# Row-wise infinity norm of an 8192 x 8192 matrix: another cut of the rows into transfers, and another way out for the results

## The chip, the cores and the metric

The kernel runs on one core of a Trainium2 chip; the other cores are idle. The metric is the device time of one execution in microseconds, and the number compared is the median of several executions. A separate execution is recorded by the hardware profiler; all durations below are from that one.

## The reference

```python
def setup_inputs():
    return {
        "x": np.random.randn(8192, 8192).astype(np.float32),
    }

def reference(x: np.ndarray) -> np.ndarray:
    return np.linalg.norm(x, ord=np.inf, axis=1)
```

With `axis=1` the infinity norm of a row is the largest absolute value in it. So 268.4 MB are read, one maximum is taken over each row of 8192 numbers, and 8192 numbers (32 KB) are written.

## The kernel before

The 8192 rows are laid over the 128 partitions of SBUF, so that each partition holds 64 rows ("row slots" below). They come in groups `g` of 256 rows, and partition `p` of a group holds rows `2p` and `2p+1` of it: the view `x_g` (line 53) makes these two rows one run of 16384 numbers (64 KB, contiguous in DRAM). In this text a column is one float32 in each of the 128 partitions, 512 bytes in all; the input has 524288 columns.

`_pieces` cuts these columns into 47 transfers: 25 whole pairs of rows (16384 columns), then, from the list `TAIL`, eight single rows (8192), and fourteen pieces that shrink from 6400 to 1408 columns. A piece never crosses a pair, but it may cross the border between the two rows of one.

Every piece is one DMA, issued by SyncE (line 81), into a ring of three pairs (`RING`, 49152 columns). A piece that doesn't fit before the ring's end starts at 0 again. The framework makes the DMA wait until the reduces that read the old contents of its place are done. In the program as built, the DMAs take eight completion semaphores in turn, so a DMA also waits for the landing of the one that last used its semaphore.

VectorE takes the pieces in the same order. `absmax` (line 66) is one `tensor_reduce` with maximum of absolute values. Whole rows in a piece give their result straight to `res`; a part of a row gives a partial maximum to `part`, and when the row's last part is in, a second small `tensor_reduce` (line 98) joins the partial results into `res`.

When the last pair but one is done (line 103), the 62 results of each partition are brought into DRAM order: for each of the two rows of a pair, TensorE transposes 31 columns of `res` into PSUM with the identity (line 108), ScalarE copies them to `o_sb` (line 109), and ScalarE issues two stores (lines 111 and 112). The results of the last pair go straight from `res` to DRAM at the very end, by a store on SyncE's queue (line 113): 128 partitions with 8 bytes each.

No order is written out by hand other than that of the program text; each engine runs its own list, and semaphores join the lists.

Of the kernel before, what the change touches and what calls it, by code (L numbers as in the profile page):

```python
# [1 line left out]

# [5 lines left out]

P = 128
FP32 = mybir.dt.float32  # L10

TAIL = (
    [8192] * 8
    + [6400, 5888, 4096]
    + [4992, 4544, 3776, 3072]
    + [3264, 2944, 2624, 2304, 2112, 1728, 1408]
)
RING = 3 * 16384  # L20


def _pieces(total, n_cols, pair):

    tail = sum(TAIL)
    assert (total - tail) % pair == 0
    cuts = [(a, a + pair) for a in range(0, total - tail, pair)]
    at = total - tail
    for w in TAIL:
        end = at + w  # L30
        while at < end:
            e = min(end, (at // pair + 1) * pair)
            cuts.append((at, e))
            at = e
    return cuts


@with_exitstack
def kernel(
    ctx: ExitStack,  # L40
    tc: tile.TileContext,
    x: bass.AP,
    out: bass.AP,
):
    nc = tc.nc
    n_rows, n_cols = x.shape
    R = 2
    pair = R * n_cols
    G = n_rows // (P * R)
    total = n_rows // P * n_cols  # L50


    x_g = x.rearrange("(g p r) m -> g p (r m)", p=P, r=R)
    out_g = out.rearrange("(g p r) -> g p r", p=P, r=R)

    single = ctx.enter_context(tc.tile_pool(name="single", bufs=1))
    psum_pool = ctx.enter_context(tc.tile_pool(name="psum", bufs=1, space=bass.MemoryType.PSUM))

    ring = single.tile([P, RING], FP32)
    res = single.tile([P, G, R], FP32)  # L60
    part = single.tile([P, G * R, 8], FP32)
    ident = single.tile([P, P], FP32)
    make_identity(nc, ident)

    def absmax(dst, src):
        nc.vector.tensor_reduce(  # L66
            out=dst, in_=src, axis=mybir.AxisListType.X,
            op=mybir.AluOpType.max, apply_absolute_value=True,
        )

    n_part = {}
    flushed = False
    at = 0
    for a, b in _pieces(total, n_cols, pair):
        w = b - a
        if at + w > RING:
            at = 0
        g = a // pair
        buf = ring[:, at : at + w]
        at += w  # L80
        nc.sync.dma_start(out=buf, in_=x_g[g, :, a - g * pair : b - g * pair])
        s = a
        while s < b:
            row = s // n_cols
            if s % n_cols == 0 and b - s >= n_cols:
                k = (b - s) // n_cols
                absmax(
                    res[:, g, row % R : row % R + k],
                    buf[:, s - a : s - a + k * n_cols].rearrange("p (k m) -> p k m", m=n_cols),
                )  # L90
                s += k * n_cols
                continue
            e = min(b, (row + 1) * n_cols)
            i = n_part.get(row, 0)
            n_part[row] = i + 1
            absmax(part[:, row, i : i + 1], buf[:, s - a : e - a])
            if e == (row + 1) * n_cols:
                nc.vector.tensor_reduce(  # L98
                    out=res[:, g, row % R : row % R + 1], in_=part[:, row, : i + 1],
                    axis=mybir.AxisListType.X, op=mybir.AluOpType.max,  # L100
                )
            s = e
        if b == (G - 1) * pair and not flushed:
            flushed = True
            o_sb = single.tile([G - 1, P, R], FP32)
            for r in range(R):
                o_ps = psum_pool.tile([G - 1, P], FP32, name=f"o_ps{r}")
                nc.tensor.transpose(o_ps, res[:, : G - 1, r], ident)  # L108
                nc.scalar.copy(o_sb[:, :, r], o_ps)  # L109
            h = (G - 1) // 2 + 1  # L110
            nc.scalar.dma_start(out=out_g[:h], in_=o_sb[:h])
            nc.scalar.dma_start(out=out_g[h : G - 1], in_=o_sb[h:])
    nc.sync.dma_start(out=out_g[G - 1], in_=res[:, G - 1, :])


# [1 line left out]
_INS = ['x']  # L117
_OUTS = [((8192,), 'float32')]


# [23 lines left out]
```

## Time and profile before

| | us |
|---|---|
| median of 7 executions | 632.41 |
| lowest, highest | 632.0, 633.05 |
| the profiled execution's own time | 632.0 |
| its span (first to last instruction) | 630.2 |
| VectorE busy, share of the span | 552.2, 88% |
| DMA packets of the loads, share of the 16 DMA engines' span | 98.8% |
| mean rate | 426 GB/s |
| TensorE, ScalarE, GpSimd busy | 0.8, 1.8, 0.7 |

The span is a little shorter than the time of the same execution: 1.8 us lie outside it. A busy share is an average over the whole run; where the run's end is set must be read from the stage at the end. The chain of waits follows the last instruction back to whatever released it. Windows give the busy time of each engine in a stretch of the run.

### The profile page before, as it was taken

The numbers are of one execution on the slowest core, as the hardware profiler recorded it, in microseconds if no ns is written. First come the engines' busy times: TensorE is split into PE (matmuls) and PEld (weight loads), VectorE is DVE, ScalarE is ACT, GpSimd is POOL, SyncE is SP. The second block draws the span as 40 slices with busy tenths as digits, with TensorE's granted clock in tenths as the row PEclk, the third lists the DMA queues.
The fourth block names the chain that finished last, engine by engine and source line by source line (L and its number), as shares of the span: only waits on it lengthen the run. The fifth ranks groups of instructions, "written<-read, shape, count | busy, mean of one in ns | idle before, by whom it ended". The sixth has DMA issues, their size and how long they took to land.

```text
span 630.2 us, 200 instructions
## 1 busy us (share of the span) xinstructions
PE 0.8 (0%) x2; PEld 0.3 (0%) x2; DVE 552.2 (88%) x56; ACT 1.8 (0%) x3; POOL 0.7 (0%) x6
## 2 busy tenths in 40 slices
PE   0000000000000000000000000000000000000000
PEld 0000000000000000000000000000000000000000
DVE  0588988889988889888899888898888999999997
ACT  0000000000000000000000000000000000000000
POOL 0000000000000000000000000000000000000000
DMA  9999999999999999999999999999999999999995
GB/s 399 412 453 428 437 441 424 453 412 453 412 462 404 466 399 466 399 466 399 466 399 466 399 466 399 466 399 466 399 466 399 433 433 433 433 437 422 425 423 225
DMA packets 6975, 268.48 MB, mean 426 GB/s; under 512 B 927, under 2 KB 958, under 8 KB 1214
## 3 DMA queue, kind: packets, MB, share of 16 engines
q1 hardware_dynamic: 6912, 268.44, 98.8%
q10 hardware_dynamic: 62, 0.03, 0.0%
q14 instruction: 1, 0.01, 0.0%
HBM read 268.44 MB, written 0.03 MB: 426 GB/s over the span
## 4 chain that ended last, share of the span: by engine, by line
DMA 62%; DVE 37%; issue 0%
DMA ring<-in_x_dram 62%; DVE res L66 29%; DVE part L66 8%; DVE res L98 0%
## 5 line engine op out<-in xcount | busy, mean ns | idle before, releaser
L66 DVE TENSOR_REDUCE res<-ring 128x2 f32<-128x16384 f32 (+1 forms) x33 | 499.3, 15149 | 74.1 <-DMA ring<-in_x_dram 74.1
L66 DVE TENSOR_REDUCE part<-ring 128x1 f32<-128x4096 f32 (+15 forms) x17 | 52.6, 3155 | 0.0
L109 ACT COPY o_sb<-o_ps 31x128 f32<-31x128 f32 x2 | 0.5, 262 | 606.9 <-PE o_ps L108 606.9
L108 PE MATMUL o_ps<-ident,res 128*31 128x128 f32 x2 | 0.8, 407 | 608.3 <-DVE res L98 608.3
L109 ACT ACT_TABLE_LOAD x1 | 1.3, 1283 | 0.7 <-PEq L128 0.7
L98 DVE TENSOR_REDUCE res<-part 128x1 f32<-128x2 f32 (+2 forms) x6 | 0.9, 151 | 0.1
L108 PEld LDWEIGHTS o_ps<-ident,res 128*31 128x31 f32 x2 | 0.3, 128 | 608.6 <-issue 601.3
masks.py:199 POOL TENSOR_SCALAR_AFFINE_SELECT ident<-ident 128x128 f32<-128x128 f32 x1 | 0.3, 292 | 0.1
masks.py:197 POOL MEMSET ident<- 128x128 f32 x1 | 0.2, 204 | 0.3 <-POOLq L128 0.3
L128 POOL MEMSET const-bfloat16-1.0<- 128x1 bf16 x1 | 0.1, 102 | 0.0
L128 POOL MEMSET const-uint8-127<- 128x1 uint8 x1 | 0.1, 102 | 0.0
L128 POOL MEMSET const-float32-0.0<- 128x1 f32 x1 | 0.1, 99 | 0.2 <-issue 0.2
L128 POOL MEMSET const-float32-1.0<- 128x1 f32 x1 | 0.1, 99 | 0.0
## 6 DMA issues: line engine op xcount, KB each, us to landing
ring<-in_x_dram SPq DMA_DIRECT2D x8, 4096.0 KB, 40.5
ring<-in_x_dram SPq DMA_DIRECT2D x1, 3200.0 KB, 42.3
ring<-in_x_dram SPq DMA_DIRECT2D x1, 2944.0 KB, 40.7
ring<-in_x_dram SPq DMA_DIRECT2D x1, 2496.0 KB, 42.9
ring<-in_x_dram SPq DMA_DIRECT2D x1, 2272.0 KB, 39.8
ring<-in_x_dram SPq DMA_DIRECT2D x1, 2048.0 KB, 45.2
ring<-in_x_dram SPq DMA_DIRECT2D x1, 1888.0 KB, 44.0
ring<-in_x_dram SPq DMA_DIRECT2D x1, 1632.0 KB, 43.3
```

Of the source, the lines that this page charges most:

```text
L66: nc.vector.tensor_reduce(out=dst, in_=src, axis=mybir.AxisListType.X, op=mybir.AluOpType.max, apply_absolute_value=True,)
L98: nc.vector.tensor_reduce(out=res[:, g, row % R : row % R + 1], in_=part[:, row, : i + 1], axis=mybir.AxisListType.X, op=mybir.AluOpType.max,)
L108: nc.tensor.transpose(o_ps, res[:, : G - 1, r], ident)
L109: nc.scalar.copy(o_sb[:, :, r], o_ps)
L128: nc = _bacc.Bacc("TRN2", target_bir_lowering=False, num_devices=1)
```

## The change

The 64 row slots are now cut in another order and another way. Four single rows come first (each partition one row of 32 KB), then 23 pairs in one transfer each, then five pairs in two or three pieces, then four single rows in 2, 3, 4 and 6 pieces, the last of them 896 columns wide. That makes 53 loads. A single row slot is 128 consecutive rows of the input, one to a partition, where before every slot was half of a pair. Results of pairs are slots 0 to 55 of `res`, results of single rows are 56 to 63.

Only slots below 48 write a whole row's result straight to `res`. All slots from 48 to 62 write to `part`, which has room for four partial results each and is filled with zeros by GpSimd at the start; one `tensor_reduce` (128 x 15 results out of 128 x 60) joins them all, after the last piece of the last row but one. The small joins of before are gone.

After that join come the stores of slots 0 to 62: three transposes on TensorE (28, 28 and 7 columns), three copies and two stores on ScalarE. In the program as built, ScalarE makes all three copies and then issues both stores.

The last row's first five pieces write their partial maxima into five columns behind the space in which its last piece lands (`last`, 901 columns), so that one reduce over the whole of `last` gives the row's result `fin`. `fin` (128 partitions, one number each) is transposed by TensorE into one partition, copied from PSUM to SBUF by VectorE, and stored by SyncE as one run of 512 bytes.

```diff
-TAIL = (
-    [8192] * 8
-    + [6400, 5888, 4096]
-    + [4992, 4544, 3776, 3072]
-    + [3264, 2944, 2624, 2304, 2112, 1728, 1408]
-)
+HEAD = 4
+PAIRS = 28
+PIECES = (
+    [[8192]] * HEAD
+    + [[16384]] * 23
+    + [[8192, 8192], [7232, 9152], [6720, 9664], [8640, 7744], [5568, 5568, 5248]]
+    + [[4480, 3712], [3392, 1920, 2880], [2752, 1600, 2048, 1792]]
+    + [[1792, 1664, 1472, 1280, 1088, 896]]
+)
 RING = 3 * 16384
...
+CUT = 48
+K = 4
...
-    res = single.tile([P, G, R], FP32)
-    part = single.tile([P, G * R, 8], FP32)
+    res = single.tile([P, R - 1], FP32)
+    part = single.tile([P, R - 1 - CUT, K], FP32)
+    nc.gpsimd.memset(part, 0.0)
...
+    n_last = len(PIECES[-1]) - 1
+    w_last = PIECES[-1][-1]
+    last = single.tile([P, w_last + n_last], FP32)
+    fin = single.tile([P, 1], FP32)
...
+    def singles_out():
+        n = R - 1 - X_ONE
+        ps = psum_pool.tile([n, P], FP32, name="ps_singles")
+        sb = single.tile([n, P], FP32, name="sb_singles")
+        nc.tensor.transpose(ps, res[:, X_ONE:], ident)
+        nc.scalar.copy(sb, ps)
+        nc.scalar.dma_start(
+            out=out[X_ONE * P : (R - 1) * P].rearrange("(r p) -> r p", p=P), in_=sb
+        )
+
+    def pairs_out():
+        sb = single.tile([PAIRS, P, 2], FP32, name="sb_pairs")
+        both = res[:, :X_ONE].rearrange("p (g r) -> p g r", r=2)
+        for r in range(2):
+            ps = psum_pool.tile([PAIRS, P], FP32, name=f"ps_pairs{r}")
+            nc.tensor.transpose(ps, both[:, :, r], ident)
+            nc.scalar.copy(sb[:, :, r], ps)
+        nc.scalar.dma_start(
+            out=out[: X_ONE * P].rearrange("(g p r) -> g p r", p=P, r=2), in_=sb
+        )
...
+    next_pair, next_one = 0, X_ONE
+    for u, widths in enumerate(PIECES):
+        k = sum(widths) // n_cols
+        if k == 2:
+            row, next_pair = next_pair, next_pair + 2
+        else:
+            row, next_one = next_one, next_one + 1
+        src = x[row * P : (row + k) * P].rearrange("(p r) m -> p (r m)", r=k)
...
+            nc.sync.dma_start(out=buf, in_=src[:, off : off + w])
+            if final:
+                absmax(fin[:, :1], last)
+                break
...
+                if c and r + c <= CUT:
+                    absmax(
+                        res[:, r : r + c],
+                        buf[:, s : s + c * n_cols].rearrange("p (c m) -> p c m", m=n_cols),
+                    )
...
+                if r == R - 1:
+                    absmax(last[:, w_last + i : w_last + i + 1], buf[:, s:e])
+                else:
+                    absmax(part[:, r - CUT, i : i + 1], buf[:, s:e])
...
-                nc.tensor.transpose(o_ps, res[:, : G - 1, r], ident)
-                nc.scalar.copy(o_sb[:, :, r], o_ps)
-            h = (G - 1) // 2 + 1
-            nc.scalar.dma_start(out=out_g[:h], in_=o_sb[:h])
-            nc.scalar.dma_start(out=out_g[h : G - 1], in_=o_sb[h:])
-    nc.sync.dma_start(out=out_g[G - 1], in_=res[:, G - 1, :])
+        if u == len(PIECES) - 2:
+            nc.vector.tensor_reduce(
+                out=res[:, CUT:], in_=part, axis=mybir.AxisListType.X, op=MAX,
+            )
+            pairs_out()
+            singles_out()
+
+    fin_ps = psum_pool.tile([1, P], FP32)
+    fin_sb = single.tile([1, P], FP32)
+    nc.tensor.transpose(fin_ps, fin, ident)
+    nc.vector.tensor_copy(out=fin_sb, in_=fin_ps)
+    nc.sync.dma_start(out=out[(R - 1) * P :].rearrange("(r p) -> r p", p=P), in_=fin_sb)
```

More of the change, by code (lines that the diff above doesn't have):

```diff
@@ L10 @@
 FP32 = mybir.dt.float32
-TAIL = (
-    [8192] * 8
-    + [6400, 5888, 4096]
-    + [4992, 4544, 3776, 3072]
-    + [3264, 2944, 2624, 2304, 2112, 1728, 1408]
+MAX = mybir.AluOpType.max
+HEAD = 4
[6 more added lines that the diff above has]
+    + [[1792, 1664, 1472, 1280, 1088, 896]]
 )
 RING = 3 * 16384
[L23 to L35, printed above, removed]
+CUT = 48
+K = 4
 @with_exitstack
@@ L46 @@
     n_rows, n_cols = x.shape
[L47 to L54, printed above, removed]
+    R = n_rows // P
+    assert R == 64 and n_cols == 8192
+    X_ONE = 2 * PAIRS
     single = ctx.enter_context(tc.tile_pool(name="single", bufs=1))
@@ L59 @@
     ring = single.tile([P, RING], FP32)
-    res = single.tile([P, G, R], FP32)
-    part = single.tile([P, G * R, 8], FP32)
+    res = single.tile([P, R - 1], FP32)
+    part = single.tile([P, R - 1 - CUT, K], FP32)
+    nc.gpsimd.memset(part, 0.0)
     ident = single.tile([P, P], FP32)
     make_identity(nc, ident)
+    n_last = len(PIECES[-1]) - 1
+    w_last = PIECES[-1][-1]
+    last = single.tile([P, w_last + n_last], FP32)
+    fin = single.tile([P, 1], FP32)
     def absmax(dst, src):
         nc.vector.tensor_reduce(
-            out=dst, in_=src, axis=mybir.AxisListType.X,
-            op=mybir.AluOpType.max, apply_absolute_value=True,
-        )
@@ L71 @@
-    n_part = {}
-    flushed = False
-    at = 0
[L74 to L89, printed above, removed]
-                )
[L91 to L107, printed above, removed]
-                nc.tensor.transpose(o_ps, res[:, : G - 1, r], ident)
-                nc.scalar.copy(o_sb[:, :, r], o_ps)
-            h = (G - 1) // 2 + 1
-            nc.scalar.dma_start(out=out_g[:h], in_=o_sb[:h])
-            nc.scalar.dma_start(out=out_g[h : G - 1], in_=o_sb[h:])
@@ L113 @@
-    nc.sync.dma_start(out=out_g[G - 1], in_=res[:, G - 1, :])
+            out=dst, in_=src, axis=mybir.AxisListType.X, op=MAX, apply_absolute_value=True,
+        )
+    def singles_out():
[7 more added lines that the diff above has]
+        )
@@ new lines @@
+    for u, widths in enumerate(PIECES):
[5 more added lines that the diff above has]
+        src = x[row * P : (row + k) * P].rearrange("(p r) m -> p (r m)", r=k)
+        off = 0
+        n_part = {}
+        for h, w in enumerate(widths):
+            final = u == len(PIECES) - 1 and h == n_last
+            if final:
+                buf = last[:, :w]
+            else:
+                if at + w > RING:
+                    at = 0
+                buf = ring[:, at : at + w]
+                at += w
+            nc.sync.dma_start(out=buf, in_=src[:, off : off + w])
+            if final:
+                absmax(fin[:, :1], last)
+                break
+            s = 0
+            while s < w:
+                r = row + (off + s) // n_cols
+                left = n_cols - (off + s) % n_cols
+                c = (w - s) // n_cols if left == n_cols else 0
+                if c and r + c <= CUT:
[3 more added lines that the diff above has]
+                    )
+                    s += c * n_cols
+                    continue
+                e = min(w, s + left)
+                i = n_part.get(r, 0)
+                n_part[r] = i + 1
+                if r == R - 1:
+                    absmax(last[:, w_last + i : w_last + i + 1], buf[:, s:e])
+                else:
+                    absmax(part[:, r - CUT, i : i + 1], buf[:, s:e])
+                s = e
+            off += w
+        if u == len(PIECES) - 2:
[4 more added lines that the diff above has]
+            singles_out()
```

## The prediction

> **What bounds the kernel now.** I read the windows first, to see whether the loads ever pause, then SyncE's waits, then the chain of waits for the end, then the timeline and the stores. Windows (columns: length, busy of PE, PEld, DVE, ACT, POOL, granted clock, DMA share, GB/s):
>
> ```profile
> 22.65:487.00 464.35, 0.00 (x0) 0.00 (x0) 413.28 (x24) 0.00 (x0) 0.00 (x0) 1.00 1.00 432
> 487.00:565.00 78.00, 0.00 (x0) 0.00 (x0) 77.60 (x9) 0.00 (x0) 0.00 (x0) 1.00 1.00 432
> 565.00:624.05 59.05, 0.81 (x2) 0.26 (x2) 58.98 (x22) 0.52 (x2) 0.00 (x0) 1.00 0.98 416
> 624.05:630.20 6.15, 0.00 (x0) 0.00 (x0) 2.34 (x3) 0.00 (x0) 0.00 (x0) 1.00 0.01 0
> ```
>
> The DMA engines are full until 624, so 620 us are a stream that only fewer bytes or less overhead could shorten. SyncE's waits:
>
> ```profile
> SPq L81 <- DVE res L66: 478.7, 31, 17.2
> SPq L81 <- DMA ring<-in_x_dram: 110.4, 32, 20.6
> ```
>
> Loads wait to be issued, but a pair takes 40.8 us from issue to landing at one landing per 19.35 us: another load is always queued ahead, and those waits cost nothing. The end of the chain (start, length, what):
>
> ```profile
> 487.06 34.42 DVE res L66 x3
> 521.48 0.02 issue
> 521.49 43.25 DMA ring<-in_x_dram
> 564.74 0.03 issue
> 564.77 8.69 DVE res L66
> ...
> 618.13 8.11 DVE part L66 x4
> 626.24 0.03 issue
> 626.27 0.16 DVE res L98
> ```
>
> From 564.77 on VectorE never pauses. The last load was issued at 608.1 and took 15.9 us (DMA issues), so it landed at 624.0; its reduce began at 624.62. VectorE is 0.6 us behind at the end. What follows the last byte is small, as the timeline and the stores' own view show:
>
> ```profile
> 608.54 9.52 DVE L66 TENSOR_REDUCE part<-ring 128x1 f32<-128x3264 f32 x4
> 618.04 8.19 DVE L66 TENSOR_REDUCE part<-ring 128x1 f32<-128x2304 f32 x4
> 626.27 0.16 DVE L98 TENSOR_REDUCE res<-part 128x1 f32<-128x5 f32 x1
> 626.45 0.35 SPq L113 DMA_DIRECT2D out_dram<-res  x1
> ```
> ```profile
> DMA to landing us min/median/max: 2.7/4.7/5.0
> ```
>
> The 2.7 is the final store: issue 626.45, landing 629.18, then 1.0 us of closing barrier to 630.2.
>
> **Prices.** *Loads.* In the trace's packet records the last packets of successive pairs are 19.35 us apart, those of successive single rows 9.71. Twice 9.71 less 19.35 is 0.07 per transfer; 9.64 per 8192 columns remains. The 1728-column piece fits: 2.03 + 0.07 = 2.10, recorded 2.12. *Reduces.* 8192 columns take 8.676 us, 1408 take 1.612: 1.0417 ns a column and 0.143. Back to back only some 0.06 shows: 2304, 2112, 1728 and 1408 make 7552 columns, 7.87 + 0.143 + 3 x 0.06 = 8.19, as recorded. A reduce that waits for the one before shows the 0.143 and 0.03 more.
>
> **What the Trainium skill says.** "VectorE: DVE Perf Modes", on the TRN2 errata, has each SBUF-source instruction pay a fixed cost whatever its size; the trace agrees (0.143). "DMA: Bandwidth & Descriptors", in the anatomy of one DMA, puts most of a small transfer's fixed 2 us down to the receipt of the last write. The trace agrees: the final store's packets are over by 627.49, yet its sixteen completions come between 627.70 and 629.18. The same page, on why a DMA increments its semaphore by 16, lets the slowest dimension that isn't 1 set the number of engines; whether a 1 x 128 store goes as one run of 512 bytes or sixteen of 32, no row here shows. Its section on latency lists row pitches from 512 KiB up as slow; it says nothing of the 32 and 64 KB of this case.
>
> **The change, part by part.**
>
> *Loads.* 53 for 47: 6 x 0.07 = +0.41. The same bytes. The queue stays fed: a load waits for reduces three pairs back, as before, and in the tail for the landing of an earlier load with over 8 us of loads still queued. The other delays I carry over: 0.34 from 599.74, where an 8 KB instruction fetch in the packet records sets one DMA engine back, and 0.08 where ScalarE's stores pass. The last load lands at 624.02 + 0.41 = 624.4.
>
> *Singles first, zeros by GpSimd.* The first reduce starts near 13 (half the first transfer) instead of 22.66, but VectorE then waits for the stream anyway (2.13 us at each pair before): nothing. GpSimd's fill lies under the first load. Opening transfers of half the size might shorten the ramp: the first packets took 3.2 us against 2.42 later. I take 0, bounded by -0.4 and 0.
>
> *VectorE's tail.* From landing of the last whole pair (487.2) VectorE has that pair, five split pairs and four rows: 131072 columns, 136.5 us, with 35 reduces, so 2.1 of gaps. I set landing against end of the reduce before, piece by piece. VectorE stays behind throughout, by 0.3 to 7 us; the single join costs 0.24, of which nothing is hidden. At the end the pieces 1472, 1280, 1088, 896 land at 620.3, 621.9, 623.3, 624.4 and begin at 620.7, 622.3, 623.7, 625.0. The last reduce takes 901 x 1.0417 ns + 0.143 = 1.08 and ends at 626.1. Before, the final join ended at 626.43: -0.33. The change thus trades a narrower last piece (-0.53) and a missing final join (-0.16) against one longer load stream (+0.41) and about the same lag. Bounds: -0.3 where it hides better, +0.4 where a few gaps are longer.
>
> *ScalarE's stores.* They start after the join, near 617, not at 609.4. Three transposes and three copies (about 0.4 and 0.26 each), two issues (0.38, 0.67), 5.0 to landing: all landed by about 624. The final chain ends after 628, which hides it; without that cover up to 1 us would be exposed.
>
> *Result of the last row.* New on the path: TensorE's transpose and VectorE's copy. Before, from the end of line 98 to the end of line 108 took 0.54 and 0.48 (wait, weights, 0.39 to 0.42 matmul): 0.52. A copy of 128 numbers by ScalarE took 0.26: 0.26 for VectorE. Nothing stands behind either. So SyncE issues at 626.1 + 0.78 + 0.03 = 626.9, which is +0.45 against 626.45.
>
> *The store itself.* 128 writes of 8 bytes become one run. From issue to first packet 0.85 passed; the first completion came 0.36 after its packet. Lower bound 0.85 + 0.05 + 0.4 = 1.3; upper bound the 2.72 of before, or 3.0 if the issue takes ScalarE's 0.67 rather than 0.35. I take 1.7, since the wait before was for the slowest of sixteen receipts. Saved: 1.0.
>
> *Sum.* +0.45 - 1.0 = -0.55 (bounds -0.95 - 0.4 - 0.3 = -1.65 and +0.45 + 0.3 + 0.4 = +1.15). Profiled: 632.0 - 0.55 = 631.45; that run was the lowest of the seven, so on the median 632.41 - 0.55, about 631.8.
>
> **Rivals.**
>
> *The store does best and the ramp shrinks.* Store 1.3, ramp -0.4: -0.55 - 0.8 = -1.35, so 631.0. For it: the slowest receipts are 1.5 us later than the fastest. Against: the trace has no small store without others beside it.
>
> *The store is no cheaper.* Then only the added 0.45 stays, up to 0.75 with the long issue: 632.9 to 633.2. For it: the receipt, not the data, makes up the 2.7.
>
> *Single rows stream slower.* The four rows in front and four behind are now read with 32 KB between partitions, never so read in the trace. They are 65536 columns, 77 us. From 1.26 + 0.55 = 1.8 us on, which is 2.4% of it (a 32 KB packet of 1.245 us instead of 1.215), the kernel is slower by over 0.2%; at 3.5% it takes 632.41 - 0.55 + 2.7 = 634.6. Against: runs of 32 KB at 64 KB pitch came at the pairs' rate.
>
> *The change doesn't do what it says.* It speaks of a transpose on VectorE and 128 byte runs; the code has TensorE and 512. That is what was priced.
>
> **How the numbers follow.** 0.2% (1.26 us) is what a measurement of this kernel can tell from no change. Forecast 0.43 (631.8; own range 631.3 to 632.3). Best store and ramp 0.30 (631.0). Store no cheaper 0.14 (632.9). Slow single rows 0.13 (634.6). The range 630.7 to 633.2 leaves out the slow rows (0.13) and the last of the faster cases, below the sum's lower bound of -1.65 or close to it (about 0.05); it takes in both bounds of the store. The first rival is faster by over 0.2%: 0.30. The forecast and the dear store lie within: 0.57. Slower: 0.13.
>
> **What would show it.** Last landing near 624.4, the last reduce ending near 626.1, SyncE's store issued near 626.9 and landed in 1.7; VectorE without a pause from 487 on. A pause in the tail would say that the loads came late; a 32 KB packet over 1.22 us in the first four loads, or a store over 2.7, would make the forecast wrong.

## The result and the profile after

The changed kernel takes 630.62 us (median of 14 executions, 630.44 to 630.84) against 632.32 for the kernel before (34 executions, 631.98 to 633.05): a ratio of 0.9973, 95% interval 0.9966 to 0.998. That is 1.70 us less, where 0.55 was forecast, and 0.08 below the stated range. The first rival, the best store, lies nearest. The profiled execution took 630.57, span 628.8.

The timeline of the changed kernel at its end (start, length, engine, line, operation, out<-in, idle time before):

```profile
616.84 0.22 DVE L134 TENSOR_REDUCE res<-part 128x15 f32<-128x60 f32 x1
616.97 7.98 DVE L63 TENSOR_REDUCE last<-ring 128x1 f32<-128x1792 f32 x5
618.12 0.61 ACTq L84 DMA_DIRECT2D out_dram<-sb_pairs  x1
618.82 0.28 ACTq L73 DMA_DIRECT2D out_dram<-sb_singles  x1
624.99 1.09 DVE L63 TENSOR_REDUCE fin<-last 128x1 f32<-128x901 f32 x1
626.13 0.08 PEld L142 LDWEIGHTS fin_ps<-ident,fin 128*1 128x1 f32 x1 [8.63 <-DVE fin L63]
626.13 0.37 PE L142 MATMUL fin_ps<-ident,fin 128*1 128x128 f32 x1 [8.14 <-DVE fin L63]
626.54 0.28 DVE L143 COPY fin_sb<-fin_ps 1x128 f32<-1x128 f32 x1 [0.46 <-PE fin_ps L142]
626.85 0.32 SPq L144 DMA_DIRECT2D out_dram<-fin_sb  x1
```

The last reduce ends at 626.08, where before the last join ended at 626.43: the new cut of the rows is 0.34 ahead there. Then come transpose and copy, and the store is issued at 626.85, 0.40 later than before. So at the issue of the store the changed kernel is behind. The chain of waits (start, length, what) shows what led there:

```profile
487.22 34.41 DVE res L63 x3
521.62 95.19 DVE part L63 x22
616.82 0.03 issue
616.84 0.22 DVE res L134
617.06 7.91 DVE last L63 x5
624.97 0.02 issue
624.99 1.10 DVE fin L63
```

From 487.22 to the last reduce no load appears: VectorE is never idle. The last load lands in that time, as the issues of the changed kernel (last column: us from issue to landing) and the view of the tile `last` say, 614.3 + 10.1 = 624.4:

```profile
last<-in_x_dram SPq DMA_DIRECT2D x1, 448.0 KB, 10.1
```
```profile
L108 SPq DMA_DIRECT2D last<-in_x_dram x1: 328/328/328, 614.3 to 614.3; - x1
```

The loads thus ended 0.4 later than before and VectorE is 0.6 behind them, as it was. So the whole gain lies behind the store's issue. SyncE's closing wait for the store (us, times, longest), first of the kernel before, then of the changed one:

```profile
SPq L139 <- DMA out_dram<-res: 2.3, 1, 2.3
```
```profile
SPq L170 <- DMA out_dram<-fin_sb: 0.5, 1, 0.5
```

The store landed 1.11 us after its issue instead of 2.72 (626.85 to 627.96; landed means that the last of its completions is in the trace's records). The closing part, from the landing to the end of the span, took 0.83 instead of 1.00: SyncE looks at the completion semaphores two at a time, about 0.065 us each look. Before, three such looks came after the store's (629.24, 629.30 and 629.36); the changed kernel's store is on the pair looked at last, so that the others are done by then. The sum for the profiled executions: +0.40 - 1.61 - 0.17 = -1.38, and the spans differ by 630.175 - 628.789 = 1.39.

### The profile page after: what moved, and what is told of

The parts are those of the page before. It is cut to its first block, busy times and chain, and to the rows that moved or that the text cites. A ratio compares the mean times of both kernels' runs of the same rounds, so it can differ in the third digit from the quotient of the medians.

```text
span 628.8 us, 217 instructions
## 1 busy us (share of the span) xinstructions
PE 1.2 (0%) x4; PEld 0.3 (0%) x4; DVE 552.7 (88%) x59; ACT 2.0 (0%) x4; POOL 0.8 (0%) x7
## 4 chain that ended last, share of the span: by engine, by line
DMA 57%; DVE 43%; issue 0%; SPq 0%; PE 0%
DMA ring<-in_x_dram 57%; DVE res L63 25%; DVE part L63 17%; DVE last L63 1%; DVE fin L63 0%; SPq L108 0%; PE fin_ps L142 0%; DVE fin_sb L143 0%; DVE res L134 0%
## 5 line engine op out<-in xcount | busy, mean ns | idle before, releaser
L63 DVE TENSOR_REDUCE res<-ring 128x2 f32<-128x16384 f32 (+1 forms) x25 | 413.2, 16537 | 57.5 <-DMA ring<-in_x_dram 57.5
L63 DVE TENSOR_REDUCE part<-ring 128x1 f32<-128x8192 f32 (+19 forms) x26 | 130.0, 5066 | 16.1 <-DMA ring<-in_x_dram 16.1
L63 DVE TENSOR_REDUCE last<-ring 128x1 f32<-128x1792 f32 (+4 forms) x5 | 8.0, 1662 | 0.0
```

The lines of the kernel that those rows point to most:

```text
L63: nc.vector.tensor_reduce(out=dst, in_=src, axis=mybir.AxisListType.X, op=MAX, apply_absolute_value=True,)
```

## Experiments

All runs are compared with the kernel before on the same chip; its medians there lay between 632.42 and 632.59. Two theories stood against each other. A: the way out made the gain, through the store's landing. B: the new cut of the rows and the late join made it.

**The new cut with the old way out.**

```diff
-    fin_ps = psum_pool.tile([1, P], FP32)
-    fin_sb = single.tile([1, P], FP32)
-    nc.tensor.transpose(fin_ps, fin, ident)
-    nc.vector.tensor_copy(out=fin_sb, in_=fin_ps)
-    nc.sync.dma_start(out=out[(R - 1) * P :].rearrange("(r p) -> r p", p=P), in_=fin_sb)
+    nc.sync.dma_start(out=out[(R - 1) * P :].rearrange("(p o) -> p o", o=1), in_=fin)
```

> The changed kernel, but the last row's result goes straight from fin to DRAM (128 partitions, 4 bytes each, as the kernel before did with 8), without transpose and copy. Theory A (the store's landing is what the change gained): the store is issued 0.77 us earlier, near 626.1, but lands after about 2.7 us instead of 1.11, and the closing waits take 0 to 0.2 longer; 630.62 + 1.6 - 0.77 + 0.1, so about 631.5 (631.3 to 631.9). Theory B (the new cut of the rows and the late join gained it): no slower than the changed kernel, 629.9 to 630.6.

Measured: 636.61 us, ratio 1.0064 (1.0051 to 1.0077), slower than the kernel before. Timeline, SyncE's waits and the stores' view (last line: shortest, median, longest us from issue to landing) of this run:

```profile
625.19 1.09 DVE L63 TENSOR_REDUCE fin<-last 128x1 f32<-128x901 f32 x1
626.30 0.35 SPq L140 DMA_DIRECT2D out_dram<-fin  x1
```
```profile
SPq L166 <- DMA out_dram<-fin: 7.1, 1, 7.1
```
```profile
DMA to landing us min/median/max: 7.8/7.8/7.8
```

The issue came earlier, as expected, but the store took 7.8 us, far beyond both theories. Its packets were over by 627.35; the sixteen completions came between 630.23 and 634.07. B falls as the main cause: up to the issue the new cut was worth 0.15 in this execution (626.30 for 626.45). One number for each partition, stored as 4 bytes, is nearly three times as dear as the 8 bytes of before, so a last row alone in its slot needs another way out.

**The old cut with the new way out.** In the kernel before:

```diff
-    nc.sync.dma_start(out=out_g[G - 1], in_=res[:, G - 1, :])
+    fin_sb = single.tile([1, P, R], FP32)
+    for r in range(R):
+        fin_ps = psum_pool.tile([1, P], FP32, name=f"fin_ps{r}")
+        nc.tensor.transpose(fin_ps, res[:, G - 1, r : r + 1], ident)
+        nc.vector.tensor_copy(out=fin_sb[:, :, r], in_=fin_ps)
+    nc.sync.dma_start(out=out_g[G - 1 : G].rearrange("g p r -> g (p r)"), in_=fin_sb.rearrange("g p r -> g (p r)"))
```

> The kernel before with its own cut and joins; only the last pair's results are transposed by TensorE into one partition (two transposes, two copies by VectorE) and stored as one run of 1024 bytes. Theory A: issue about 1.1 us later, landing 1.1 after it instead of 2.7 or more: 632.32 + 1.1 - 1.6 to 1.9, so 631.5 to 631.8. Theory B: the way out is only a cost, about 633.0 to 633.4.

Measured: 631.92, ratio 0.9993 (0.9985 to 1.0001), so no gain that is clear of no change. The store took 1.12 us, but VectorE's copy of the first row had been put between its big reduces. The timeline of this run:

```profile
618.37 0.14 DVE L98 TENSOR_REDUCE res<-part 128x1 f32<-128x3 f32 x1
618.98 0.28 DVE L117 COPY fin_sb<-fin_ps 1x128 f32<-1x128 f32 x1 [0.47 <-PE fin_ps L116]
619.19 8.18 DVE L66 TENSOR_REDUCE part<-ring 128x1 f32<-128x2304 f32 x4
```

VectorE waited 0.47 for TensorE there, and the next reduce began 0.75 later than it would have, on an engine with no slack. So the copy went to ScalarE:

```diff
-        nc.vector.tensor_copy(out=fin_sb[:, :, r], in_=fin_ps)
+        copy = nc.vector.tensor_copy if r == R - 1 else nc.scalar.copy
+        copy(out=fin_sb[:, :, r], in_=fin_ps)
```

> As the run that gave the kernel before only the new way out, but the first of its two small copies is made by ScalarE, so that it no longer stands between VectorE's big reduces, where it cost 0.75 us of waiting. Theory A: 631.92 - 0.75, about 631.2 (631.0 to 631.4); the rest of the way to 630.62 is then the cut of the rows and the late join. If the stall was not on the path: 631.9.

Measured: 631.54, ratio 0.9984 (0.9977 to 0.9991), 0.4 better rather than 0.75. In the profiled execution, one of the longest of its 19 (631.98), the stall was gone, but the last load landed at 624.70, later than in the first of these two (624.33). The way out alone thus gives about 0.9 of the 1.7 us on the old cut. The changed kernel's own profile has the same share: 0.74 more from the last reduce to the issue, 1.61 less from there to the landing, which is 0.87. What is left of its 1.39 is 0.34 from the new cut with the late join, 0.17 from the closing part, and rounding.

**The late join undone.** In the changed kernel:

```diff
+                if r != R - 1 and e - s == left and n_part[r] > 1:
+                    nc.vector.tensor_reduce(
+                        out=res[:, r : r + 1], in_=part[:, r - CUT, : i + 1],
+                        axis=mybir.AxisListType.X, op=MAX,
+                    )
...
-                if c and r + c <= CUT:
+                if c:
...
-            nc.vector.tensor_reduce(
-                out=res[:, CUT:], in_=part, axis=mybir.AxisListType.X, op=MAX,
-            )
```

> The changed kernel, but each row's partial results are joined as soon as its last part is in, as the kernel before did: eight small joins between the big reduces, and no late join. Theory A (VectorE runs without a pause from 487 us to the end, so anything added to it in the tail is paid in full): eight joins of about 0.2 us less the late join's 0.35: 1.2 us slower, about 631.8. Rival (its lag behind the loads hides them): 630.5 to 630.8.

Measured: 631.43, ratio 0.9981 (0.9974 to 0.9988). The profiled execution was the longest of the 17 (631.72). From its groups and its timeline:

```profile
L132 DVE TENSOR_REDUCE res<-part 128x1 f32<-128x2 f32 (+2 forms) x8 | 1.2, 151 | 0.2
```
```profile
487.50 34.41 DVE L63 TENSOR_REDUCE res<-ring 128x2 f32<-128x16384 f32 x3 [2.13 <-DMA ring<-in_x_dram]
626.14 1.09 DVE L63 TENSOR_REDUCE fin<-last 128x1 f32<-128x901 f32 x1
```

The last reduce begins 1.15 later than with the late join (626.14 for 624.99). Of this 0.28 was there at the last whole pair (487.50 for 487.22), before any join; the eight joins in place of the one cost 0.87. Between the medians it is 0.8. VectorE's pieces follow each other without a pause from 487.50 on, and although the last load landed 0.48 later than in the changed kernel (624.88), the last reduce began 1.27 after it. So in this stretch the joins are paid in full, and this is the clearest sign that VectorE sets the time there.

**VectorE relieved.** `absmax2` takes the place of `absmax` for all partial maxima in `part` and `last`. It leaves out the absolute value, so its results are other numbers:

```diff
+    dump = single.tile([P, 4096], mybir.dt.bfloat16)
+
+    def absmax2(dst, src):
+        n = src.shape[1] // 2
+        nc.vector.tensor_tensor_reduce(
+            out=dump[:, :n], in0=src[:, :n], in1=src[:, n : 2 * n], scale=1.0, scalar=0.0,
+            op0=mybir.AluOpType.mult, op1=MAX, accum_out=dst,
+        )
```

> The changed kernel, but every partial maximum is taken in one pass over two halves of the piece at once, as the maximum of their products: this leaves out the absolute maximum itself, and takes about half of VectorE's time in the tail. Theory A (VectorE's work from 487 us on sets when the last reduce begins, 0.6 us after the last landing): the last reduce begins within 0.1 to 0.2 of the landing, 0.4 to 0.5 faster, 630.1 to 630.2. If the loads alone set it: 630.6.

Measured: 630.60, ratio 0.9969 (0.9957 to 0.9982), no gain over the changed kernel. The timeline of this run:

```profile
623.96 0.73 DVE L71 CUSTOM_DVE_ANT_0 dump<-ring 128x544 bf16<-128x544 f32 x1 [0.49 <-DMA ring<-in_x_dram]
624.61 0.08 DVE L71 DVE_READ_ACCUMULATOR2_ANT last<- 128x1 f32 x1
624.99 1.09 DVE L63 TENSOR_REDUCE fin<-last 128x1 f32<-128x901 f32 x1 [0.30 <-DMA last<-in_x_dram]
```

VectorE now waits for the loads and begins 0.09 after the last landing. But that landing is at 624.90 instead of 624.39. In the packet records the loads lose 0.3 and 0.5 us near 570, where this longer program (two instructions a piece) has one more 8 KB instruction fetch; the second delay has no record beside it. The time is the one expected if the loads alone set it, but the trace shows one limit taken away and the other moved; what the lag alone is worth stays open.

**Shrinking earlier, with a wider last piece.**

```diff
-    + [[16384]] * 23
-    + [[8192, 8192], [7232, 9152], [6720, 9664], [8640, 7744], [5568, 5568, 5248]]
-    + [[4480, 3712], [3392, 1920, 2880], [2752, 1600, 2048, 1792]]
-    + [[1792, 1664, 1472, 1280, 1088, 896]]
+    + [[16384]] * 22
+    + [[9408, 6976], [9152, 7232], [7488, 8896], [8384, 8000], [8704, 7680]]
+    + [[6656, 6016, 3712]]
+    + [[4416, 3776], [2688, 3456, 2048], [1856, 2624, 1664, 2048]]
+    + [[2112, 1792, 1536, 1408, 1344]]
...
-CUT = 48
+CUT = 44
```

> The changed kernel with one pair more cut in two (22 whole pairs, six split ones) and the last row in five pieces ending with 1344 columns instead of six ending with 896; 53 loads as before. Worked out piece by piece from the recorded durations, VectorE's lag at the end shrinks from 0.6 to about 0.1, the last reduce is 0.47 longer, its end 0.2 to 0.25 earlier: 630.4 (630.3 to 630.6). If VectorE's lag didn't matter: 631.1.

> The changed kernel itself, beside the two others on the same chip: 630.6, last reduce beginning 0.6 us after the last landing, store 1.1 us.

Measured: 631.07, ratio 0.9977 (0.9968 to 0.9987), beside 630.56, ratio 0.9969 (0.9957 to 0.9981), for the changed kernel. The timeline of the recut run:

```profile
625.08 1.56 DVE L64 TENSOR_REDUCE fin<-last 128x1 f32<-128x1348 f32 x1 [0.31 <-DVE last L64]
```

The last load landed at 624.57, so VectorE was half a microsecond behind still: 0.31 of it is idle time that no load or other engine's record explains. The reduce itself is 0.47 longer, which is what the prediction's price per column gives for 447 columns more. The trade tried here was a loss. The time, 631.07, is the one expected if VectorE's lag didn't matter; but as the lag shrank by only 0.1 us, this run doesn't tell.

**Pairs in front.**

```diff
-PAIRS = 28
+PAIRS = 30
...
-    [[8192]] * HEAD
-    + [[16384]] * 23
+    [[16384]] * 25
...
-CUT = 48
+CUT = 52
```

> The changed kernel with 25 whole pairs in front instead of four single rows and 23 pairs (51 loads instead of 53, all results of slots 0 to 51 direct, 52 to 62 joined late); the tail is the same. Theory A: the order in front costs or gains nothing but the two loads less, 0.07 us each: 630.4 to 630.8. Theory C (half-sized opening transfers shorten the ramp): 0.2 to 0.4 slower, 630.8 to 631.0 or more.

Measured: 631.08, ratio 0.9978 (0.9969 to 0.9987), whose interval overlaps the changed kernel's. The numbers are those that theory C named, but the trace doesn't bear it out: the last reduce begins only 0.1 later than in the changed kernel (625.09), and its store lands 0.1 later. The rest of the 0.57 in span lies behind: the store is now on a semaphore looked at third of five, and one of VectorE's closing sequencer instructions comes some 0.4 late for a reason that no record shows. The opening itself shows no gain: the first 16384 columns had arrived by 22.19 to 22.50 in the seven recorded executions with pairs in front, and by 22.23 to 22.64 in the nine with single rows.

**What makes the store short.** A1: the store of before waits for the slowest of sixteen completions. A2: fewer and longer writes. A3: tiny writes into one stretch of DRAM hold each other up.

```diff
-        out=out[(R - 1) * P :].rearrange("(r p) -> r p", p=P), in_=fin_sb
+        out=out[(R - 1) * P :].rearrange("(o a b) -> o a b", o=1, a=16),
+        in_=fin_sb.rearrange("o (a b) -> o a b", a=16),
```

> The changed kernel, with the final 512 bytes sent from the same partition as 16 runs of 32 bytes, which 16 DMA engines can share. Theory A1 (one receipt instead of the slowest of sixteen makes the store short): the store takes 1.5 to 2.7 us again, 631.0 to 632.2. Theory A2 (fewer and longer writes make it short, the number of engines doesn't matter): 1.1 to 1.3 us, 630.5 to 630.8.

Measured: 630.57, ratio 0.997 (0.9959 to 0.9981). It tells nothing of A1: the packet records hold one packet of 512 bytes, so the sixteen runs were joined again before they reached the engines.

```diff
-    fin = single.tile([P, 1], FP32)
+    fin = single.tile([P, 32], FP32)
+    nc.gpsimd.memset(fin, 0.0)
...
-    fin_ps = psum_pool.tile([1, P], FP32)
-    fin_sb = single.tile([1, P], FP32)
-    nc.tensor.transpose(fin_ps, fin, ident)
-    nc.vector.tensor_copy(out=fin_sb, in_=fin_ps)
-    nc.sync.dma_start(out=out[(R - 1) * P :].rearrange("(r p) -> r p", p=P), in_=fin_sb)
+    fin_t = single.tile([P, 32], FP32)
+    nc.vector.transpose(fin_t, fin)
+    nc.sync.dma_start(
+        out=out[(R - 1) * P :].rearrange("(a b) -> a b", b=32), in_=fin_t[0:P:32, :]
+    )
```

> The changed kernel, with fin transposed by VectorE in blocks of 32 x 32 (a 128 x 32 tile, zeros beside the result) and stored from four partitions as four runs of 128 bytes, in place of TensorE's transpose, the copy and one run of 512 bytes. Theory A1 (slowest of the receipts): the path to the issue shrinks from 0.77 to about 0.25, the store grows from 1.11 to some 1.2 to 1.5 with four receipts: 630.2 to 630.5. Theory A2: store 1.1, 630.1. If a store of four short runs costs as much as the 128 of before: 631.7.

Measured: 630.72, ratio 0.9971 (0.9961 to 0.9982). The timeline of this run:

```profile
626.09 0.21 DVE L142 STREAM_TRANSPOSE fin_t<-fin 128x32 f32<-128x32 f32 x1
626.32 0.65 SPq L143 DMA_DIRECT2D out_dram<-fin_t  x1
```

The path from the reduce's end to the issue shrinks to 0.27, as expected. But to issue a store from four partitions took 0.65 instead of 0.32, and the first packet came 1.25 instead of 0.75 after its start, so that it landed at the same moment (627.96). An instruction fetch of 0.50 ran meanwhile (from 626.12); whether it held the issue up no record shows. The completions came within 0.07 of each other: four of them cost nothing.

The next three change only the final store of the kernel before. It now sends all 64 columns of `res` from each partition in one run, or the last eight, or the last four. What they leave out is the reference's order of the results; they are there for the store's time alone. The edit of the first:

```diff
-    nc.sync.dma_start(out=out_g[G - 1], in_=res[:, G - 1, :])
+    nc.sync.dma_start(out=out.rearrange("(p c) -> p c", p=P), in_=res.rearrange("p g r -> p (g r)"))
```

> The kernel before, but its final store sends, from each of 128 partitions, one run of 256 bytes (all of res, over the whole output, so the order of the results is not the reference's). Same 128 writes over sixteen DMA engines as before, 32 times the bytes, none of them near another. Theory A1 (the slowest of sixteen receipts makes the store of before long): 2.7 us or more, 632.3 or more. Theory A3 (many tiny writes into the same stretch of DRAM hold each other up): 1.1 to 1.5 us, 630.7 to 631.3.

> The kernel before, but its final store sends one run of 32 bytes from each partition (eight columns of res into the first 4 KB of the output, so the order of the results is not the reference's). Theory A1: as e8, 632.3. Theory A3: between the 256 byte runs and the 8 byte runs, 1.3 to 2.0 us, 631.0 to 632.0.

> The kernel before, with one run of 16 bytes from each partition in its final store (four columns of res into the first 2 KB of the output, so the order of the results is not the reference's). Theory A3 (the write's size decides, below 32 bytes it gets dear): 1.5 to 2.2 us, 631.1 to 632.0. If 32 bytes is no border and only 4 and 8 byte writes are dear by their number in one stretch: 1.4 us, 630.9.

Measured: 630.85, 630.96 and 630.83, ratios 0.9974 (0.9964 to 0.9984), 0.9974 (0.9964 to 0.9983) and 0.9976 (0.9966 to 0.9985). The stores' view of the 16 byte run (its shortest is the final store):

```profile
L113 SPq DMA_DIRECT2D out_dram<-res x1: 347/347/347, 626.6 to 626.6; - x1
DMA to landing us min/median/max: 1.4/4.8/5.1
```

Issue to landing of the final store in all these runs, from the completion records:

| bytes of one run | runs | us |
|---|---|---|
| 4 | 128 | 7.77 |
| 8 (the kernel before) | 128 | 2.72 |
| 16 | 128 | 1.41 |
| 32 | 128 | 1.42 |
| 256 | 128 | 1.46 |
| 128 | 4 | 1.64 |
| 512 (the changed kernel) | 1 | 1.11 |
| 1024 | 1 | 1.12 |

A1 falls: with 256 byte runs all sixteen completions come within 0.17 us, though as many writes run over as many engines. What is dear is 128 writes of 4 or 8 bytes; at 16 bytes the cost is gone, so 32 bytes is no border, as one theory of the 16 byte run had it. A single run of 512 or 1024 bytes saves another 0.3. In all these stores the runs lie side by side in DRAM, so their size and their distance changed together. Eight byte writes far apart were not tried, and whether size alone or the crowding that A3 names makes them dear stays open. How the memory handles the small writes no record shows.

**A version without the transpose.** If 16 or 32 bytes from each partition do, the results needn't leave by TensorE. In the changed kernel the eight single row slots become eight neighbouring rows of each partition. The store in the last lines takes the place of `singles_out` and of the transpose, copy and store at the end:

```diff
-        src = x[row * P : (row + k) * P].rearrange("(p r) m -> p (r m)", r=k)
+        if k == 2:
+            src = x[row * P : (row + k) * P].rearrange("(p r) m -> p (r m)", r=k)
+        else:
+            src = x[X_ONE * P :].rearrange("(p r) m -> r p m", p=P)[row - X_ONE]
...
-                absmax(fin[:, :1], last)
+                absmax(res[:, R - 1 :], last)
...
+    nc.sync.dma_start(
+        out=out[X_ONE * P :].rearrange("(p r) -> p r", p=P), in_=res[:, X_ONE:]
+    )
```

> The changed kernel, but the eight single row slots hold eight neighbouring rows in each partition (rows 7168 + 8p to 7168 + 8p + 7), so that their eight results leave as one run of 32 bytes from each partition straight out of res; no transpose, copy or separate store for them. Theory A with A3: the store is issued 0.75 us earlier and takes 1.4 instead of 1.1, closing waits 0.07 longer: 0.4 faster, about 630.2. Rival (single rows read with 256 KB between partitions stream slower): 631 or more, with packets of 32 KB above 1.22 us.

Measured: 630.13 us, ratio 0.9965 (0.9953 to 0.9978), the lowest of all medians. The timeline of this run:

```profile
624.89 1.09 DVE L62 TENSOR_REDUCE res<-last 128x1 f32<-128x901 f32 x1
626.01 0.35 SPq L131 DMA_DIRECT2D out_dram<-res  x1
```

The issue is 0.84 earlier, the store takes 1.42, and it lands at 627.43 instead of 627.96. The bytes of each single row in front take 9.68 us in the packet records, as in the changed kernel, although the partitions now read 256 KB apart: the rival of the slow single rows doesn't hold for these sizes. The gain over the changed kernel is 0.5 by the medians and by the spans; the intervals of the two ratios overlap, so the times alone don't show it.

## Why the prediction was wrong

**The loads: right.** Last landing forecast 624.4, recorded 624.39. The 0.07 for each added transfer fits, and so does the carried-over delay from the instruction fetch (0.3 near 589 here). That it fits to the hundredth is luck: with the same loads as before, six recorded executions have the last landing at 624.02 to 624.70.

**VectorE's tail: right.** Last reduce forecast to end at 626.1, recorded 626.08. VectorE never paused from 487 on. The small joins run showed that its work there counts in full. One count was off: the working has 35 reduces in this stretch, the trace has 31 and the join. The 2.1 for the gaps came out all the same (138.86 from 487.22 to 626.08, less 136.5 for the columns and 0.24 for the join), because a gap was 0.07 rather than 0.06.

**ScalarE's stores: right.** Issued at 618.1 and 618.8, landed by 623.2, hidden behind the final chain.

**Transpose and copy: right.** 0.77 from the reduce's end to the store's issue, forecast 0.78 + 0.03; issue at 626.85, forecast 626.9.

**The store itself: the step that failed.** "Lower bound 0.85 + 0.05 + 0.4 = 1.3 ... I take 1.7, since the wait before was for the slowest of sixteen receipts." It took 1.11. The direction was right, but the term was mis-sized by 0.59, and its lower bound wasn't one. The first packet started 0.75 after the issue, not 0.85; 0.85 is what the stores from 128 partitions show, here too. The completion came 0.33 after its packet. And the reason was wrong: not the number of receipts, but 128 writes of only 8 bytes made the store of before long, as the runs with 16 to 256 bytes show. With 1.11 in place of 1.7 the profiled sum is -1.16; 0.17 more is the closing part, taken as unchanged, and the remaining 0.05 is the issue, forecast at +0.45 and recorded at +0.40.

The section of the Trainium skill that the prediction cites for the receipt ("DMA: Bandwidth & Descriptors", the anatomy of one DMA) puts about 2 us on a small transfer, most of it the receipt, and describes transfers that GpSimd issues. SyncE's store of one run took 1.11 in all, and only 0.33 of it came after the packet; for this store the measurement decides.

**The base.** The forecast took a difference worked out on one profiled execution off a median. The profiled one of before, 632.0, was near the lowest of its kernel, whose executions spread over 1.1 us; those of the changed kernel spread over 0.4. By the profiles the gain is 632.0 - 630.57 = 1.43, by the medians 1.70. That the 8 byte store takes longer in most executions than in the profiled one would explain the 0.3, and fits the runs with 16 to 256 byte runs, which are 1.5 to 1.6 faster by the medians where their stores are 1.3 shorter. It is argued, not shown: only one execution of the kernel before was recorded. A rival is that this execution had early loads: its last landing at 624.02 is the earliest of the six recorded executions with the old cut, and the next two, at 624.04 and 624.16, belong to executions 0.08 and 0.04 below their medians. The runs that gave the old cut another way out, without an 8 byte store, spread over 0.7 as well. How much of the 0.3 belongs to which stays open.

**The rivals.** The best store and a shorter ramp gave 631.0, near the result, but half of it for a wrong reason: there was no gain at the ramp. "The store is no cheaper" is refuted by every run whose final store has runs of 16 bytes or more, and its bound from above was harmless only because 8 bytes became 512: with 4 bytes the store took 7.8. Slow single rows: a packet of 32 KB took 1.21 to 1.22 us once the stream ran, as before.

## What to carry to other kernels

A store that ends a kernel is worth measuring by the size of its pieces: here 128 pieces of 4 or 8 bytes cost 7.8 and 2.7 us, pieces of 16 bytes 1.4, one piece 1.1. Before transposing results on chip to get longer runs, see whether the rows can be dealt to the partitions so that four neighbouring results lie side by side. And where an engine has had no pause for a hundred microseconds, look for small instructions among its work: here one copy cost 0.75 us with the wait before it, and eight joins cost 0.87 more than one.

## What the runs showed of the hardware that was not expected

- 128 runs of 4 bytes: the packets were over in 0.2 us, but their completions came 2.9 to 6.7 us later. With 8 bytes it was 0.2 to 1.7, with 16 bytes and more at most 0.4.
- A 1 x 128 store left as one packet of 512 bytes on one DMA engine, even when written as 16 runs. The prediction had left this open.
- Issuing a store took SyncE 0.32 us from one partition, 0.65 from four and 0.35 from 128, and ScalarE 0.28 from seven and 0.61 from 28: not in order of size.
- An 8 KB instruction fetch took one DMA engine 0.3 us, and all later landings were late by about as much. It came at another time in another program: near 600 with the old cut, near 589 in the changed kernel, at 569 and again at 589 in the longer program with VectorE relieved.
